# Inside the group or between two groups: where a small product, its decays and the sample fetches are placed in a hybrid recurrent step

## The chip, the cores and the metric

The kernel runs on one core of one Trainium2 chip. The metric is the device time of one execution in microseconds. Three runs of the kernel before gave 994.37, 994.74 and 998.79 us, median 994.74 us. A further execution was profiled, and every row of the trace comes from that one; its own time and its span are in the table below. One core has five engines with queues of their own: TensorE (PE, with its weight loads as PEld), VectorE (DVE), ScalarE (ACT), GpSimd (POOL) and SyncE (SP), which here only issues DMAs.

## The reference, cut to what matters

One step of a decoder trunk of two layers, for 256 prompt tokens and 8 sample sequences of 8 tokens, in float32:

```python
# layer 0
proj = einsum('btd,de->bte', rmsnorm(x), w_in)       # 2048 -> qkv, b, a, z_a, q_b, k_b, v_b, lr_b, z_b
qkv  = silu(causal_conv4(qkv, conv_a))               # 3072 columns
beta = sigmoid(b_raw); g = -exp(a_log) * softplus(a_raw + dt_bias)
o_a, S_a = gated_delta_rule(q_a, k_a, v_a, g, beta, S_a)          # 8 heads, chunked
gk   = log_sigmoid(einsum('btr,rk->btk', lr_b, w_lr) + b_lr) / 16
o_b, S_b = gla(q_b, k_b, v_b, gk, S_b)                            # 4 heads, chunked
x   += einsum('bte,ed->btd', concat(norm(o_a)*silu(z_a), norm(o_b)*silu(z_b)), w_out)
# layer 1
x   += RG-LRU(conv4(w_x rmsnorm(x))) * silu(w_g rmsnorm(x)) @ w_out
return rmsnorm(x), all new states (delta, gla, lru, conv) of prompt and samples
```

Three parts of this matter here. The narrow columns of `w_in`, 16 of `lr_b` and 8 each of `b_raw` and `a_raw`, make a product 32 columns wide, the small group. From it come the gates `g` and `beta` of the delta rule and, over `w_lr`, the decays `gk` of the gated linear attention (GLA). And every sample sequence has a state of its own (8 sequences x 8 heads of 128x128 for delta, x 4 heads of 128x256 for GLA), which is read, updated with the sample's keys and values, and written back.

## The kernel before, in words

**The dense products.** All 320 tokens (256 prompt, 64 sample) lie as columns, features on the 128 partitions. The wide weights are cut into groups of 512 output columns; a group has 8 weight loads of 512 KB (`wst`, three buffers) and four accumulators `acc` in PSUM of 128x320. Each weight tile is split into a rounded part `wh` (L239, ScalarE) and a rest `wl` (L240, VectorE), each input into `xh` and `xl`, and multiplied in three matmuls: xh with wh, xh with wl, xl with wh (L264). There are 5760 such matmuls; where the text says "a product" or counts products, it means one of them. When a group's accumulator is complete, its `evac` reads it out: for the groups of the convolution VectorE multiplies by the row scale `rb` into `slab` (L354, L355, `evac_padded`), and four taps make `yc` (L463). `rb` is 1/rms of each token; it comes from a chain over all of `x` (`start_work`, `row_rstd`, with L342 and L346), and some of the constants for it and for later come in `tables` (`pa`, `pc`, `dta`, `pb`, over SP's queue).

**What sets the order.** `run_group` walks the products; between them it calls `slot`, which lets one step of each work queue go on: `hi`, `lo` and `tails` hold generators, and a generator's `wait("name")` lets as many slots pass as the table `WAITS` says. The order of the instructions of each engine follows from where the generators' steps fall between the products, and from priorities that a scheduler uses on top. SP's DMAs are tied to the last product before them by `behind`.

**The border of groups 2 and 3.** (Groups counted from 1.) After the second group the program lets `hi` run until the row scale is in use ("start" done), then calls `small_group()`: 16 float32 matmuls of 32 columns into `smacc` (L490, 32 records in the trace), and on VectorE `sm` (L492, and a copy L494). The pool `start_p` is closed, and `lo` receives `small_work()` and behind it `gla_decays()`. `small_work` transposes `sm` (`smt`, L503), makes the gates, sums them up over the tokens with six short matmuls (`cum`, L533 to L538) and takes exponentials. `gla_decays` makes `gk`: `sml` (L1188), `lrp`, exponentials, a scan. Being behind `small_work` in the same queue, it starts when that has ended.

**The samples.** `sample_states` runs over the heads. `fetch` (L996) loads the rows for the update from scratch in DRAM into a tile of 96 partitions, three copies of the same 32 rows, by one DMA with a source of [0, 3], [4w, 32], [1, n*w]: `uk` and `uv` (192 KB) for delta, `uvk` (288 KB) for GLA. VectorE casts them (L1003), GpSimd takes the rests (L1007) and spreads them over four sequences (`uvm`, L1012), TensorE multiplies (`sn` L1112 for delta, `gsn` L1126 for GLA) and VectorE adds to the state (`ust` L1116, `ugt` L1130).

**GLA's output** goes through `gla_out`: squares on ScalarE (L1164), a power on GpSimd (`gso`), `gon` on VectorE (L1169), two transposes `got` on TensorE (L1173).

The functions and the calls:

Of the kernel before, what the change touches and what calls it, by code (L numbers as in the profile page):

```python
# [65 lines left out]
def wait(name):  # L66
    for _ in range(WAITS[name]):
        yield
# [3 lines left out]
def hybrid_step(ctx, tc, x_cols, w_dense, w_small, w_lr, w_gate, par_a, par_b, par_c, gains, head_rows,  # L72
# [3 lines left out]
    pe, act, dve, pool, sp = nc.tensor, nc.scalar, nc.vector, nc.gpsimd, nc.sync  # L76
# [36 lines left out]
    hi, lo, tails = [], [], []  # L113

    def advance(queue):
        while queue:
            try:
                next(queue[0])
                return True
            except StopIteration:  # L120
                queue.pop(0)
        return False
# [3 lines left out]
    def behind(i):  # L126
        tc.add_manual_dep(i.ins, marks[-1].name, mybir.DependencyInfo(
            mybir.DependencyClass.NoSync, mybir.DependencyReason.DATA), reason="issue_after")
# [12 lines left out]
    def slot0(n_lo=1):  # L141
        advance(hi)
        for _ in range(n_lo):
            advance(lo)
        advance(tails)

    def drain(queue):
        while advance(queue):
            pass
# [267 lines left out]
    def until(flag):  # L417
        while flag not in env["done"]:
            assert advance(lo) or advance(hi) or flag in env["done"], flag
# [76 lines left out]
    def small_work():  # L496

        yield from wait("small_work.4")
        ws = env["ws"]
# [487 lines left out]
    def sample_states(first, last):  # L987
# [5 lines left out]
        def fetch(name, src, off, n, w, bufs):  # L993

            t = ws.tile([R, n, w], F32, name=name, tag=name, bufs=bufs)
            behind(sp.dma_start(t.rearrange("p q w -> p (q w)"), bass.AP(  # L996
                tensor=src.tensor, offset=src.offset + off, ap=[[0, 3], [4 * w, 32], [1, n * w]])))
            return t
# [180 lines left out]
    def gla_decays():  # L1179

        gk = env["gk"] = env["lay0b"].tile([P, 4, NT], F32, name="gk")
# [625 lines left out]
    def shut(*pools):  # L1807
        for p_ in pools:
            p_.__exit__(None, None, None)
# [23 lines left out]
    small_group()  # L1833
    shut(start_p)
    lo.extend([small_work(), gla_decays()])
# [29 lines left out]
    drain(tails)  # L1865
    drain(lo)
# [52 lines left out]
    for m, f, n in ((0, 0, 1), (0, 1, 1), (0, 2, 2), (1, 0, 2), (1, 2, 2), (2, 0, 2), (2, 2, 2), (3, 2, 2)):  # L1919
        t = ob[m][:, f:f + n]  # L1920
# [64 lines left out]
```

## Time and profile before

| | before |
|---|---|
| runs | 994.37, 994.74, 998.79 us; median 994.74 |
| profiled execution | 994.33 us, span 992.6 us, mean granted clock 0.995 |
| TensorE busy | 969.5 us (98%) |
| VectorE, ScalarE, GpSimd busy | 707.5 (71%), 532.9 (54%), 220.2 us (22%) |
| longest groups | L264 with xh,wh 601.2, with xl,wh 595.1, with xh,wl 594.5 us (1920 matmuls each; the records overlap) |
| L240 `wl` on VectorE | 479, 726 ns each, 332.3 us |
| L239 `wh` on ScalarE | 479, 623 ns each, 278.7 us |
| DMA | 171.62 MB, mean 173 GB/s |

How to read it: busy times of matmuls are modelled and overlap, so that what TensorE really costs is read from start to start, and its idle time from the list of waits. A row of a timeline gives the start, the duration, engine, line, operation, the tile that is written and those that are read, shapes, the count, and in brackets the idle time before it with what ended that. A row of the chain of waits gives start, duration and what the end of the run was waiting for at that point.

### The profile page before, as it was taken

What the parts mean: (1) busy time and instruction counts of PE and PEld (TensorE: products, weight loads), DVE (VectorE), ACT (ScalarE), POOL (GpSimd) and SP (SyncE); (2) the same over time, 40 slices, a digit from 0 to 9 for tenths busy, and PEclk for the clock granted to TensorE, in tenths of its full rate; (3) what the DMA queues carried; (4) which work ended last, traced back from release to release, by engine and by line L of the source; (5) the groups of instructions that cost most, each with busy time, mean ns of one, the idle gap of its engine ahead of it and who ended that gap; (6) DMA issues with size and microseconds to landing.
All of it is one profiled execution on the core that took longest, in us unless ns stands there. A gap on an engine that the chain in (4) does not pass through costs nothing.

```text
span 992.6 us, 18768 instructions
## 1 busy us (share of the span) xinstructions
PE 969.5 (98%) x6917; PEld 950.5 (96%) x6917; DVE 707.5 (71%) x1485; ACT 532.9 (54%) x1083; POOL 220.2 (22%) x365
## 2 busy tenths in 40 slices
PE   9999999999999999999998999999999999999995
PEld 9989999999999999999978999999999999999995
DVE  7898887666545556779667789877969668766753
ACT  8556874457333444776423345447685885333441
POOL 4520018503282111120104234200010000052200
PEclk9999999999999999999999999999999999999998
DMA  8544444534455366445486877654545445568742
GB/s 297 178 134 135 133 130 157 143 131 135 127 157 163 93 218 228 133 111 151 157 258 204 241 258 229 228 165 146 158 124 189 130 127 169 165 216 276 258 155 106
DMA packets 64792, 171.62 MB, mean 173 GB/s; under 512 B 16345, under 2 KB 21997, under 8 KB 64189
## 3 DMA queue, kind: packets, MB, share of 16 engines
q1 hardware_dynamic: 59716, 160.35, 51.8%
q0 software_dynamic: 2720, 8.66, 2.3%
q10 hardware_dynamic: 2264, 1.42, 0.5%
q8 instruction: 54, 0.88, 0.4%
q14 instruction: 38, 0.30, 0.1%
HBM read 155.73 MB, written 14.68 MB: 172 GB/s over the span
## 4 chain that ended last, share of the span: by engine, by line
PE 44%; DVE 2%; DMA 2%; POOL 1%; issue 1%; SPq 0%; DVEq 0%; ACT 0%; POOLq 0%
PE acc L264 42%; DMA uv<-wv_scratch 1%; DMA ugt<-in_state_gla_dram 1%; POOL uvkh L1007 1%; DVE wl L240 1%; DVE ob L1921 0%; PE lg L1549 0%; PE lg L1550 0%; PE lg L1548 0%; PE gsn L1126 0%; PE sn L1112 0%; DVE xh L1410 0%; PE fsp L1670 0%; POOL gso L1166 0%; SPq L996 0%
## 5 line engine op out<-in xcount | busy, mean ns | idle before, releaser
L264 PE MATMUL acc<-xh,wh 128*128 128x320 f32 x1920 | 601.2, 313 | 2.7 <-DVE slab L355 1.2
L264 PE MATMUL acc<-xl,wh 128*128 128x320 f32 x1920 | 595.1, 310 | 1.3 <-DVE xl L1411 1.3
L264 PE MATMUL acc<-xh,wl 128*128 128x320 f32 x1920 | 594.5, 310 | 1.7 <-DVE wl L240 1.5
L239 ACT ACTIVATE wh<-wst 128x512 fp32r<-128x512 f32 x479 | 278.7, 623 | 312.5 <-PE acc L264 252.0
L240 DVE TENSOR_TENSOR wl<-wst,wh 128x512 fp32r<-128x512 f32 x479 | 332.3, 726 | 146.2 <-ACT wh L239 143.8
L264 PEld LDWEIGHTS acc<-xh,wh 128*128 128x128 f32 x1920 | 361.6, 188 | 6.0 <-issue 1.9
L264 PEld LDWEIGHTS acc<-xl,wh 128*128 128x128 f32 x1920 | 361.6, 188 | 3.4 <-DVE xl L1411 1.8
L264 PEld LDWEIGHTS acc<-xh,wl 128*128 128x128 f32 x1920 | 360.8, 188 | 3.5 <-DVE wl L240 2.8
L463 DVE SCALAR_TENSOR_TENSOR yc<-slab,pa,yc 128x344 f32<-128x344 f32 x72 | 42.6, 606 | 1.5 <-ACT yc L101 1.1
L698 POOL TENSOR_TENSOR xi<-xi,tmp 128x60 f32<-128x60 f32 (+24 forms) x62 | 26.2, 423 | 4.8
L1577 POOL MEMSET aa<- 128x32 f32 x4 | 0.7, 164 | 117.7 <-ACT rr L1564 66.7
L696 POOL TENSOR_TENSOR tmp<-ab,xi 128x60 f32<-128x60 f32 (+24 forms) x62 | 24.6, 398 | 4.9
L1007 POOL TENSOR_TENSOR uvkh<-uvk,uvkh 32x256 fp32r<-32x256 f32 (+1 forms) x8 | 12.2, 1526 | 58.3 <-DMA ugt<-in_state_gla_dram 51.0
L1012 POOL TENSOR_TENSOR uvm<-uvh,rm 96x512 fp32r<-96x512 f32 x16 | 20.9, 1327 | 1.6 <-PE sn L1112 1.3
L753 POOL TENSOR_TENSOR so<-so,mhalf 128x4 f32<-128x4 f32 x4 | 4.5, 1121 | 71.9 <-DVE so L752 71.9
L467 ACT ACTIVATE qkv<-yc 128x256 f32<-128x256 f32 x24 | 10.0, 416 | 18.7 <-DVE yc L463 18.6
L1116 DVE SCALAR_TENSOR_TENSOR ust<-ust,es,sn 128x128 f32<-128x128 f32 x64 | 17.7, 338 | 2.9 <-PE sn L1112 1.8
L101 ACT ACTIVATE yc<-slab,pa 128x344 f32<-128x344 f32 x24 | 13.3, 576 | 10.9 <-DVE slab L355 10.7
L1508 DVE SCALAR_TENSOR_TENSOR yc<-slab,pb,yc 128x344 f32<-128x344 f32 x32 | 17.5, 572 | 0.7 <-ACT yc L1506 0.6
L1119 POOL DMA_DIRECT2D out_s_delta_dram<-ust x8 | 6.0, 751 | 53.9 <-DVE ust L1116 53.9
L1130 DVE SCALAR_TENSOR_TENSOR ugt<-ugt,ebs,gsn 128x256 f32<-128x256 f32 x32 | 14.1, 472 | 4.3 <-PE gsn L1126 4.3
L354 DVE TENSOR_TENSOR slab<-acc,rb 128x256 f32<-128x256 f32 x36 | 14.9, 415 | 2.8 <-PE acc L264 2.6
(463 smaller groups left out, 1006.8 us busy)
## 6 DMA issues: line engine op xcount, KB each, us to landing
wst<-in_w_dense_dram SPq DMA_DIRECT2D x237, 512.0 KB
st<-in_state_delta_dram SPq DMA_DIRECT2D x8, 512.0 KB
st<-in_state_gla_dram SPq DMA_DIRECT2D x4, 1024.0 KB
ust<-in_state_delta_dram SPq DMA_DIRECT2D x8, 512.0 KB
out_s_delta_dram<-ust POOLq DMA_DIRECT2D x8, 512.0 KB, 5.1
ugt<-in_state_gla_dram SPq DMA_DIRECT2D x8, 512.0 KB
out_s_gla_dram<-ugt POOLq DMA_DIRECT2D x8, 512.0 KB, 5.0
x0r<-in_x_cols_dram SPq DMA_DIRECT2D x8, 320.0 KB
```

Source lines behind the costliest of these rows:

```text
L239: act.activation(h, wst[i][:, a, :], AF.Copy)
L240: env["last_split"] = dve.tensor_sub(l, wst[i][:, a, :], h.bitcast(F32))
L264: mm = pe.matmul(o, (h, h, l)[j][:, fs], (xh, xl, xh)[j][k], start=(k == 0 and j == 0), stop=(k == KT - 1 and j == 2))
L354: dve.tensor_mul(xp[:, 3:259], xp[:, 3:259] if acc is None else acc[:, :256], rb[:, :256])
L463: dve.scalar_tensor_tensor(y[:, :n], xp[:, j:j + n], pa[:, ft, j:j + 1], y[:, :n], op0=OP.mult, op1=OP.add)
L696: behind(pool.tensor_mul(tv, ab[:, j, j + 1:, None].to_broadcast([P, m, w]), xi[:, j:j + 1, :w].to_broadcast([P, m, w])))
L698: behind(pool.tensor_add(xi[:, j + 1:, :w], xi[:, j + 1:, :w], tv))
L1007: pool.tensor_sub(o, t[rows, :, cols], o.bitcast(F32))
L1012: pool.tensor_mul(m, src.bitcast(F32)[:, None, :].to_broadcast([R, 4, P]), rm4[:R, :, None].to_broadcast([R, 4, P]))
L1116: dve.scalar_tensor_tensor(s_, s_, es[:, col:col + 1], ps[:, b, :], op0=OP.mult, op1=OP.add)
L1130: dve.scalar_tensor_tensor(s_, s_, ebs[:, h, 4 * hb + b + i:4 * hb + b + i + 1], ps[:, i * 256:(i + 1) * 256], op0=OP.mult, op1=OP.add)
L1508: dve.scalar_tensor_tensor(y[:, :n], xp[:, j:j + n], pb[:, ft, 2 + j:3 + j], y[:, :n], op0=OP.mult, op1=OP.add)
```

## The change

Four things change together.

1. `small_group()` and the closing of `start_p` move out of the gap between the second and third group into `small_work()`, which begins with a new wait of 10 slots. So the 16 matmuls stand inside the third group.
2. `gla_decays()` gets a queue of its own, `lo2`, which `slot` advances once per slot beside the others. `small_work` puts it there before the first `smt`, and it begins with a new wait of 14 slots.
3. `fetch` issues three DMAs of 32 rows in place of one of 96. SP issues 36 of them where it issued 12.
4. Numbers in `WAITS`: the two new names, and other values for `small_work`, `gla_decays`, `masks`, `tables`, `sample_states`, `delta_sample`, `gla`, `quad_out`, `evac_res_sumsq`, `fill` and `resid`.

```diff
 WAITS = {
-    "small_work.1": 0, "small_work.2": 1, "small_work.3": 6,
+    "small_work.1": 0, "small_work.2": 2, "small_work.3": 10,
+    "small_work.1": 0, "small_work.2": 2, "small_work.3": 10,
-    "quad_out.1": 7, "delta_sample.7": 10, "delta_sample.5": 8,
+    "quad_out.1": 10, "delta_sample.7": 4, "delta_sample.5": 4,
-    "gla_decays.1": 16, "gla_decays.2": 8, "gla_decays.4": 10, "gla_decays.6": 0, "gla.3": 2, "gla.4": 20,
+    "gla_decays.1": 12, "gla_decays.2": 7, "gla_decays.4": 1,  "gla_decays.6": 3, "gla.3": 3, "gla.4": 16,
-    "evac_res_sumsq.1": 4, "fill.2": 14, "resid.1": 15, "sample_states.1": 9, "sample_states.14": 7,
+    "evac_res_sumsq.1": 0, "fill.2": 11, "resid.1": 7,  "sample_states.1": 8, "sample_states.14": 10,
-    "tables.1": 10, "masks.1": 5, "masks.3": 2,
+    "tables.1": 14, "masks.1": 1, "masks.3": 0, "small_work.5": 10, "gla_decays.8": 14,
...
-    hi, lo, tails = [], [], []
+    hi, lo, lo2, tails = [], [], [], []
...
         for _ in range(n_lo):
             advance(lo)
+        advance(lo2)
         advance(tails)
...
     def small_work():
 
+        yield from wait("small_work.5")
+        small_group()
+        shut(start_p)
         yield from wait("small_work.4")
+        lo2.append(gla_decays())
         ws = env["ws"]
         ps = bank("smt")
...
             t = ws.tile([R, n, w], F32, name=name, tag=name, bufs=bufs)
-            behind(sp.dma_start(t.rearrange("p q w -> p (q w)"), bass.AP(
-                tensor=src.tensor, offset=src.offset + off, ap=[[0, 3], [4 * w, 32], [1, n * w]])))
+            rows = bass.AP(tensor=src.tensor, offset=src.offset + off, ap=[[4 * w, 32], [1, n * w]])
+            for c in range(3):
+                behind(sp.dma_start(t[32 * c:32 * c + 32].rearrange("p q w -> p (q w)"), rows))
             return t
...
     def gla_decays():
 
+        yield from wait("gla_decays.8")
         gk = env["gk"] = env["lay0b"].tile([P, 4, NT], F32, name="gk")
...
     while "start" not in env["done"]:
         advance(hi)
-    small_group()
-    shut(start_p)
-    lo.extend([small_work(), gla_decays()])
+    lo.append(small_work())
```

The new lines shift the numbers: L264 is L265 in the changed kernel, L490 is L491, L996 is L1003.

What moves on the engines. First TensorE around the border of the second and third group; `xh_104` begins a group's inputs. Before:

```order
L264 MATMUL acc<-xl_135,wh 128x320
L264 MATMUL acc<-xh_119,wl 128x320
L490 MATMUL smacc<-ob_136,smw 32x320 x4
L490 MATMUL smacc<-ob_137,smw 32x320 x4
L490 MATMUL smacc<-ob_138,smw 32x320 x4
L490 MATMUL smacc<-ob_139,smw 32x320 x4
L264 MATMUL acc<-xh_104,wh 128x320
...
L264 MATMUL acc<-xh_104,wl 128x320
L503 MATMUL smt<-quart,sm 128x32 x2
L264 MATMUL acc<-xh_105,wh 128x320
```

In the change, in the third group:

```order
L265 MATMUL acc<-xl_122,wh 128x320
L265 MATMUL acc<-xh_106,wl 128x320
L491 MATMUL smacc<-ob_136,smw 32x320 x4
L491 MATMUL smacc<-ob_137,smw 32x320 x4
L491 MATMUL smacc<-ob_138,smw 32x320 x4
L491 MATMUL smacc<-ob_139,smw 32x320 x4
L265 MATMUL acc<-xh_107,wh 128x320
...
L265 MATMUL acc<-xh_107,wl 128x320
L508 MATMUL smt<-quart,sm 128x32 x3
L265 MATMUL acc<-xh_106,wh 128x320
```

The small product stood ahead of the third group's first product and now stands behind 33 of its products; nine more follow up to `smt`, where there were fifteen.

Second, VectorE from the reciprocal of the row scale (`rb_84` is rb) to the two splits around the six taps. Before:

```order
L342 RECIPROCAL rb_84<-rb_84 128x320
L240 TENSOR_TENSOR wl<-wst,wh 128x512 x3
L354 TENSOR_TENSOR slab<-slab,rb_84 128x256
L355 TENSOR_TENSOR slab<-slab,rb_84 128x8x8
L354 TENSOR_TENSOR slab<-slab,rb_84 128x256
L355 TENSOR_TENSOR slab<-slab,rb_84 128x8x8
L240 TENSOR_TENSOR wl<-wst,wh 128x512
L463 SCALAR_TENSOR_TENSOR yc<-slab,pa,yc 128x344 x6
L240 TENSOR_TENSOR wl<-wst,wh 128x512
```

In the change:

```order
L343 RECIPROCAL rb_84<-rb_84 128x320
L241 TENSOR_TENSOR wl<-wst,wh 128x512 x2
L355 TENSOR_TENSOR slab<-slab,rb_84 128x256
L356 TENSOR_TENSOR slab<-slab,rb_84 128x8x8
L355 TENSOR_TENSOR slab<-slab,rb_84 128x256
L356 TENSOR_TENSOR slab<-slab,rb_84 128x8x8
L355 TENSOR_TENSOR slab<-slab,rb_84 128x256
L241 TENSOR_TENSOR wl<-wst,wh 128x512
L464 SCALAR_TENSOR_TENSOR yc<-slab,pa,yc 128x344 x6
L241 TENSOR_TENSOR wl<-wst,wh 128x512
```

Of the splits, two instead of three stand between the reciprocal and the first slab that needs rb.

Third, SP's queue where it loads the tables; `pb` feeds `nclam`, which stands on VectorE ahead of the reciprocal. Before:

```order
L209 DMA wst<-in_w_dense_dram 128x1024
L1761 DMA pa<-in_par_a_dram 128x672
L209 DMA wst<-in_w_dense_dram 128x1024 x2
L1761 DMA pc<-in_par_c_dram 128x7
L1761 DMA dta<-in_head_rows_dram 128x16
L209 DMA wst<-in_w_dense_dram 128x1024 x2
L1761 DMA pb<-in_par_b_dram 128x688
L209 DMA wst<-in_w_dense_dram 128x1024
L1783 DMA xt_scratch<-same 128x4x128
```

In the change:

```order
L210 DMA wst<-in_w_dense_dram 128x1024
L1768 DMA pa<-in_par_a_dram 128x672
L1790 DMA xt_scratch<-same 128x4x128
L210 DMA wst<-in_w_dense_dram 128x1024 x2
L1768 DMA pc<-in_par_c_dram 128x7
L1768 DMA dta<-in_head_rows_dram 128x16
L210 DMA wst<-in_w_dense_dram 128x1024
L1768 DMA pb<-in_par_b_dram 128x688
```

`pb` comes one weight load earlier, and the scratch write of 256 KB, which came two places behind `pb`, now comes ahead of it.

More of the change, by code (lines that the diff above doesn't have):

```diff
@@ L418, in until @@
         while flag not in env["done"]:
-            assert advance(lo) or advance(hi) or flag in env["done"], flag
+            assert advance(lo) or advance(lo2) or advance(hi) or flag in env["done"], flag
     def evac_conv_a(slot_name, half, part):
@@ L1865, in hybrid_step @@
     drain(tails)
+    drain(lo2)
     drain(lo)
```

24 rows, old and new, of the table WAITS are left out of this document.

## The prediction

> **What bounds the kernel now.** I read the page's first part, then the groups of TensorE's waits, then the stretches around the longest waits, and last the chain that ended last. The page says which engine counts:
>
> ```profile
> PE 969.5 (98%) x6917; PEld 950.5 (96%) x6917; DVE 707.5 (71%) x1485; ACT 532.9 (54%) x1083; POOL 220.2 (22%) x365
> ```
>
> TensorE is busy for 98% of the 992.6 us span. The number of its instructions is the same in both kernels, so only its waits, its clock and the two ends can change. The chain gives the price of one product when nothing disturbs it, 4.41 / 30 = 0.147 us:
>
> ```profile
> 534.88 4.41 PE acc L264 x30
> ```
>
> The waits of TensorE (total us, times, longest) are the list of what can be won:
>
> ```profile
> PE got L1173 <- DVE gon L1169: 2.3, 4, 0.7
> PE acc L264 <- DVE wl L240: 1.5, 2, 0.7
> PE gsn L1126 <- POOL uvm L1012: 1.3, 1, 1.3
> PE acc L264 <- DVE xl L1411: 1.3, 2, 0.8
> PE acc L264 <- DVE slab L355: 1.2, 1, 1.2
> PE acc L264 <- DVE xh L1410: 1.1, 2, 0.8
> PE smt L503 <- DVE sm L492: 0.9, 1, 0.9
> PE cum L533 <- DVE gt L526: 0.7, 1, 0.7
> PE acc L264 <- DVE ob L1453: 0.2, 1, 0.2
> ```
>
> These add up to 10.5 us, about 1% of the run. The changed lines touch four places: the border of groups 2 and 3 (slab 1.2, smt 0.9, cum 0.7, one of the two wl waits), the first fetch of sample operands (xl, xh), the later fetches (gsn, the other wl) and, through renumbered slots, the tail of the gated linear attention (got). The clock is the fifth. In the stretches the columns are busy us of PE, PEld, DVE, ACT and POOL, then the granted clock, the DMA share and GB/s:
>
> ```profile
> 60.00:80.00 20.00, 17.73 (x136) 15.62 (x135) 18.19 (x47) 14.96 (x33) 2.90 (x6) 1.00 0.51 152
> 80.00:100.00 20.00, 19.31 (x121) 18.49 (x120) 17.16 (x51) 11.43 (x23) 0.74 (x2) 0.91 0.38 117
> ```
>
> **Part 1: the small product inside the group.** TensorE before, at the border, and VectorE, which feeds it:
>
> ```profile
> 65.06 2.36 PE L490 MATMUL smacc<-ob,smw 128*32 128x320 f32 x32
> 68.63 0.38 PE L264 MATMUL acc<-xh,wh 128*128 128x320 f32 x1 [1.21 <-DVE slab L355]
> 71.99 0.63 PE L503 MATMUL smt<-quart,sm 128*128 128x32 f32 x4 [0.93 <-DVE sm L492]
> ```
> ```profile
> 39.84 0.18 DVE L1781 TENSOR_SCALAR nclam<-pb 128x16 f32<-128x16 f32 x1 [2.34 <-DMA pb<-in_par_b_dram]
> 55.80 0.42 DVE L354 TENSOR_TENSOR slab<-slab,rb 128x256 f32<-128x256 f32 x1 [1.32 <-POOL rb L346]
> 56.74 0.69 DVE L240 TENSOR_TENSOR wl<-wst,wh 128x512 fp32r<-128x512 f32 x1
> 57.35 3.01 DVE L463 SCALAR_TENSOR_TENSOR yc<-slab,pa,yc 128x344 f32<-128x344 f32 x6
> 60.27 0.69 DVE L240 TENSOR_TENSOR wl<-wst,wh 128x512 fp32r<-128x512 f32 x1
> 67.93 0.42 DVE L354 TENSOR_TENSOR slab<-acc,rb 128x256 f32<-128x256 f32 x1
> ```
>
> The 2.36 us of small matmuls stay, 33 products later, so they cost the same. What goes is their cover: they ran while VectorE caught up with the slab that must leave PSUM before group 3 may start. The wait was 1.21 us behind that cover; without it, and with VectorE as late as now, it would be 3.6 us. How late VectorE is hangs on when the row scale rb is there (55.80). In the new order one split (L240) fewer stands ahead of that point, and that split, which TensorE needs 42 products ahead of the border (65.06 - 42 x 0.147 = 58.9), stands behind six yc. From the rb point it takes two slab pairs 0.94, half a pair 0.34, a split 0.60, the six yc 2.92 and itself 0.60: 5.4 us. If rb comes d earlier, it ends at 61.2 - d. Then follow, up to the freed bank, about 7.1 us of the same kinds (five splits 3.0, six yc 3.0, two and a quarter slab pairs 1.1): 68.3 - d.
>
> The loads of the tables move one weight load up in SP's queue, so the 2.34 us wait for pb shrinks, and the chain behind it to rb moves with it. That bounds d: 0 to 2.3. With d = 2.3 TensorE stalls nothing at the split and 1.0 at the border, together 1.0; with d = 0 it is 2.3 + 0.9 = 3.2. Then sm: in the new order ten yc (5.0), four splits (2.4), three slab pairs (1.4) stand between the first bank and sm (0.5), 9.3 us; TensorE does 42 products and the 2.36 us in that time, 8.5 us, so it waits 0.8, and up to 1.5 if the third smt waits for the copy behind sm. Against 1.21 + 0.93 = 2.1 before, the place gives -0.2 (d = 2.3, sum 1.9) to +2.4 (d = 0, smt 1.3, sum 4.5). The cum wait (0.69, one of the rows above) now has a longer lead: 0 to -0.7. The early wl wait (0.7) sits where masks and splits swap: 0 to -0.7. I take +1.1 for the place (d = 1.2) and -0.35 for each of the other two: **+0.4 us**, between -1.6 and +2.4. Outside both ends: pb might land later, since a scratch write of 256 KB also moves up; that is the rival D.
>
> **Part 2: the lane of its own for the decays.** No instruction is added on TensorE. The sml, lrp and cum matmuls keep their lengths; they only shift by tens of products, in a stretch where VectorE is at 17.16 of 20. Their work is needed only when the attention starts, many groups later, and ScalarE's one additional activation-table load has the idle 46% of that engine to lie in. Cost 0; without that cover (a waiting lrp ahead of the products on TensorE's queue) 0.7 each, the cum row's size. The stretch also holds the clock loss:
>
> ```profile
> 89.31 0.40 PE L533 MATMUL cum<-gt,umask 128*128 128x16 f32 x2 [0.69 <-DVE gt L526]
> 91.94 0.46 PE L264 MATMUL acc<-xh,wl 128*128 128x320 f32 x1
> 92.20 0.47 PE L264 MATMUL acc<-xh,wh 128*128 128x320 f32 x1
> 95.38 0.31 PE L264 MATMUL acc<-xh,wh 128*128 128x320 f32 x1
> 95.53 0.31 PE L264 MATMUL acc<-xl,wh 128*128 128x320 f32 x1
> ```
>
> Products start 0.26 us apart at 91.94 and 0.15 apart at 95.38. Over these 3.4 us some 13 products cost 0.12 each too much, 1.5 us. It follows the short cum and sml matmuls with their wait. They stay together, so I count 0, between -1.5 (gone) and +1.5 (a second such stretch). [...]
>
> **Part 3: the fetch by 32 rows.** Twelve loads become 36. The chain that ended last and VectorE's waits show what the old ones do:
>
> ```profile
> 510.55 0.80 SPq L996
> 511.39 11.29 DMA uv<-wv_scratch
> ```
> ```profile
> 522.77 0.42 DVE L1003 CAST uvh<-uv 96x512 fp32r<-96x512 f32 x1 [1.84 <-DMA uv<-wv_scratch]
> 523.11 0.32 DVE L1410 CAST xh<-ob 128x320 fp32r<-128x320 f32 x1
> 524.35 1.39 DVE L1410 CAST xh<-ob 128x320 fp32r<-128x320 f32 x1
> 871.37 0.56 DVE L1003 CAST uvkh<-uvk 96x768 fp32r<-96x768 f32 x1 [4.80 <-DMA uvk<-vk_scratch]
> ```
> ```profile
> 862.39 0.72 SPq L996 DMA_DIRECT2D uvk<-vk_scratch  x1
> L739 SPq DMA_DIRECT2D XT<-xd_scratch x16: 303/430/504, 192.0 to 309.1; - x16
> xd_scratch<-xt POOLq DMA_DIRECT2D x8, 32.0 KB, 3.3
> out_s_delta_dram<-ust POOLq DMA_DIRECT2D x8, 512.0 KB, 5.1
> ```
>
> 192 KB take 11.3 us, and 288 KB 9.0 us (862.39 to 871.37), while 512 KB elsewhere take 5.1. No 96-row load is near the others, so the shape is slow, not the size. A piece of 64 or 96 KB lies between the rows of 32 KB (3.3) and 512 KB (5.1): I take 3.5, with 5.1 as the slow end. Three issues at 0.43 each (L739) put the last piece 0.9 after the first: landing 4.4 us after the first issue, 6.0 at the slow end, instead of 9 to 11.3. SP pays 3 x 0.43 - 0.72 = 0.6 us more per fetch, 7 us in twelve places; SP mostly waits for buffers there, so 0, and 0.6 each where a weight load behind them is late. [...]
>
> At 523 to 531: uv lands near 517 instead of 522.7, VectorE's block of 1.84 us goes, and the four waits of xl and xh (2.4) with the ob wait after them shrink. They don't all go: the second xh took 1.39 instead of 0.32 while GpSimd worked beside it, and that work now comes earlier but still beside the splits. From -2.6 to 0; I take **-1.8**, since the blocked 1.84 us is the first cause in the order of time. At 879:
>
> ```profile
> 872.15 5.96 POOL L1007 TENSOR_TENSOR uvkh<-uvk,uvkh 32x256 fp32r<-32x256 f32 x2 [51.02 <-DMA ugt<-in_state_gla_dram]
> 878.18 2.35 POOL L1012 TENSOR_TENSOR uvm<-uvkh,rm 96x512 fp32r<-96x512 f32 x2
> 879.27 0.50 PE gsn L1126 x2
> ```
>
> The cast comes at 867 instead of 871.4, GpSimd's chain ends 4.6 us earlier, and gsn also stands nine products (1.3 us) later. The 1.3 us wait goes with slack: **-1.3** (0 if GpSimd really waits for ugt, which the row names; its operands are uvk alone, so I hold that for the latest semaphore). The second wl wait (0.7) lies beside the last uk and uv fetches: **-0.4**, 0 to -0.7.
>
> **Part 4: the other slots.** The four got waits come from a chain over ScalarE, GpSimd and VectorE; got and what it waits for both move by about ten products. 0 to -0.6, or +0.3 if one lands closer: **-0.2**. The tail after 970 us is not moved.
>
> **Sum.** +0.4 - 1.8 - 1.3 - 0.4 - 0.2 = -3.3 us, made against the profiled execution, 994.33 us with a span of 992.6: 991.0. The median of the runs is 0.4 above that execution; I leave 991.0.
>
> **Rivals.**
> A, the forecast: 990 to 993.5.
> B, everything moves the right way: the start ends at its good end (-1.6), all four fetch waits go (2.6 + 1.3 + 0.7 = -4.6), got -0.6, and no sparse stretch trips the clock (-1.5). -8.3, 986.0; with one or two of these missing 987 to 989. For it: each has a row that names its cause. Against it: waits on a full VectorE tend to reappear next door.
> C, the new fetches land no earlier, or GpSimd's pace and not the landing sets the waits: +0.4 - 0.2, and 0.4 saved by the later gsn: 994. For it: GpSimd's 5.96 us pair at 872; against it: 1.84 and 4.80 us of VectorE waiting for exactly these loads.
> D, slower: the row scale comes late. With VectorE at 18.19 of 20 us every us by which rb falls behind 55.80 is a us of idle TensorE, at the split and then at the border without its old cover. The cause would be pb or a weight load queued behind the 256 KB scratch write. At d = -3 the start costs +5.4 - 0.7, the fetches bring -2.5: 996.5. It eats the gains of 3.7 from d = -2 on (4.4 - 0.7), and with fetches at -2.5 the kernel would be measurably slower from d of about -6.
>
> **How the numbers follow.** About 0.5%, 5 us, is what a measurement can tell from no change: below 989.8 or above 999.7. A 0.46 (a fifth of it below 989.8), B 0.27, C 0.13, D 0.14 (0.06 of all above 999.7). Faster 0.36, same 0.58, slower 0.06. The likeliest time is 991.0. The range from 986.5 to 995.5 leaves out the best end of B and the bad half of D; A's own is 990 to 993.5.
>
> **What would show it.** Right: the gsn wait and VectorE's waits for uv and uvk are gone from their lists; the xl and xh waits are under 1 us; one new wl wait before 60 us, and 0.5 to 1.5 us at the border of group 3. Wrong: uv still lands 8 us or more after its first issue (C); rb's slab later than 55.8 us (D); granted clock 1.00 from 80 to 100 (towards B), or another stretch of 0.26 us spacing (towards D).

## The result, and the profile after

| | before | after |
|---|---|---|
| median of the runs, us | 994.56 (993.98 to 998.79, 6 runs) | 988.31 (987.04 to 989.39, 6 runs) |
| ratio, 95% interval | 1 | 0.9929 (0.9911 to 0.9947) |
| profiled execution, us | 994.33 | 988.05 |
| its span, us | 992.6 | 985.9 |

The changed kernel is faster by 6.3 us, 0.6%. The predicted 991.0 us was 2.7 us too high; the range held the time. TensorE's waits after the change (total us, times, longest; three more, at the two ends of the run, are left out, as they are in the prediction's list: they are nearly the same in both kernels):

```profile
PE acc L265 <- DVE wl L241: 3.2, 2, 2.0
PE got L1179 <- DVE gon L1175: 1.2, 2, 0.6
PE cum L538 <- DVE gt L531: 0.6, 1, 0.6
PE nbt L669 <- ACT dtm L633: 0.4, 1, 0.4
PE y L943 <- DMA XT<-xt_scratch: 0.2, 1, 0.2
```

The waits for xl, xh, ob, slab, sm and for GpSimd's uvm are gone, two of four got waits too. New are a longer wl wait and two small ones. To see where the time went, the 5760 matmuls of line L264 (L265) can be counted through in both traces: all are there, and from number 140 on in the same order (before that, 15 places hold another of the three kinds). The start times of a few of them, and below them how much each stretch got shorter or longer against before:

```
matmul no.          1500    2816    2900    3400    3600    5100    5200    5759
before, starts    268.57  517.20  533.46  609.43  641.54  875.56  892.57  977.77
after, starts     270.36  517.35  529.91  605.64  636.72  870.75  886.12  971.14

stretch          to 1500 to 2816 to 2900 to 3400 to 3600 to 5100 to 5200 to 5759
after              +1.8    -1.6    -3.7    -0.2    -1.0     0.0    -1.6    -0.2
e1 fetch only      -1.9    -0.2    -3.5     0.0    +0.2     0.0    -1.6    -0.2
e2 old fetch       +1.1    -2.0    -1.4    -0.2    -1.0     0.0    -0.3     0.0
e3 old start       -0.6    -0.7    -3.7    -0.2    -1.1     0.0    -1.6    -0.2
e6 inside, no lane +10.6   -0.3    -3.7    -0.2    -1.1     0.0    -1.6    -0.2
e7 lane only       -0.8    -2.1    -3.7    -0.2    -1.1     0.0    -1.6    -0.2
e9 inside, lane    +2.5    -2.0    -3.7    -0.2    -1.1     0.0    -1.6    -0.2
```

The first column is the start with the border of groups 2 and 3 and the delta work up to 270 us, the second the attention's tail, the third the first fetch of sample operands, the fifth the later delta fetches, the seventh the GLA fetches. The rows e1 to e9 are the experiments below. The start lost 1.8 us; every other stretch gained or stayed. Each row is one profiled execution, and the first column also differs between executions of the same code: e2 and e6 have a wait of 1.7 and 1.3 us for the first weights near 8 us, while after, with the code of e2 at that place, has none.

Two places of the trace after carry that. The start, TensorE and VectorE:

```profile
60.78 0.42 PE L265 MATMUL acc<-xh,wl 128*128 128x320 f32 x1 [2.03 <-DVE wl L241]
```
```profile
38.29 0.85 DVE L1788 TENSOR_SCALAR nclam<-pb 128x16 f32<-128x16 f32 x1
49.13 2.14 DVE L343 RECIPROCAL rb<-rb 128x320 f32<-128x320 f32 x1
55.23 0.42 DVE L355 TENSOR_TENSOR slab<-slab,rb 128x256 f32<-128x256 f32 x1 [2.29 <-POOL rb L347]
57.11 3.01 DVE L464 SCALAR_TENSOR_TENSOR yc<-slab,pa,yc 128x344 f32<-128x344 f32 x6
60.04 0.69 DVE L241 TENSOR_TENSOR wl<-wst,wh 128x512 fp32r<-128x512 f32 x1
```

pb is there 1.5 us earlier (nclam at 38.29 instead of 39.84), but rb only 0.6 us (55.23 instead of 55.80). The split behind the six yc ends at 60.7, and TensorE has waited 2.0 us for it. The granted clock in five stretches of 3.41 us around this wait and around the cum matmuls (columns as in the prediction; the clock is the third number from the end):

```profile
58.44:61.85 3.41, 1.38 (x10) 1.11 (x9) 3.41 (x10) 2.73 (x7) 0.00 (x0) 1.00 0.03 10
61.85:65.26 3.41, 3.41 (x15) 3.41 (x14) 3.41 (x8) 2.75 (x8) 0.00 (x0) 0.50 0.73 199
65.26:68.67 3.41, 3.41 (x25) 3.41 (x24) 3.41 (x9) 2.22 (x6) 2.48 (x4) 1.00 0.56 167
92.57:95.98 3.41, 2.82 (x20) 2.09 (x19) 2.80 (x11) 2.18 (x3) 0.00 (x0) 1.00 0.62 166
95.98:99.39 3.41, 3.41 (x15) 3.41 (x15) 2.84 (x6) 0.63 (x1) 0.00 (x0) 0.50 0.05 4
```

In the first stretch TensorE works 1.38 of 3.41 us; in the next it has exactly half its clock, and does 15 matmuls instead of 25. The same happens behind the cum matmuls. Before there was one such stretch, now there are two. At 0.12 us for each of 13 matmuls, as read from the rows of before, one costs 1.5 to 1.6 us (an estimate), which is most of the start's +1.8.

### The profile page after: what moved, and what is told of

It reads as the page before. It is cut to its first block, busy times and chain, and to the rows that moved or that the text cites. A ratio compares the mean times of both kernels' runs of the same rounds, so it can differ in the third digit from the quotient of the medians.

```text
span 985.9 us, 18789 instructions
## 1 busy us (share of the span) xinstructions
PE 968.4 (98%) x6917; PEld 951.9 (97%) x6917; DVE 708.9 (72%) x1485; ACT 534.7 (54%) x1084; POOL 216.6 (22%) x365
## 4 chain that ended last, share of the span: by engine, by line
PE 86%; DVE 4%; ACT 3%; issue 3%; DMA 2%; POOL 1%; SPq 0%; DVEq 0%; ACTq 0%; POOLq 0%
PE acc L265 75%; DVE wl L241 1%; ACT wh L240 1%; DMA wst<-in_w_dense_dram 1%; DMA XT<-xt_scratch 1%; DVE ob L1927 0%; POOL xsums L1782 0%; PE gpo L1368 0%; PE lg L1556 0%; PE lg L1557 0%; PE lg L1555 0%; DVE yc L464 0%; PE gsn L1132 0%; PE po L844 0%; PE sn L1118 0%
## 5 line engine op out<-in xcount | busy, mean ns | idle before, releaser
L265 PE MATMUL acc<-xh,wh 128*128 128x320 f32 x1920 | 602.0, 314 | 0.2 <-ACT wh L231 0.2
L265 PE MATMUL acc<-xh,wl 128*128 128x320 f32 x1920 | 595.2, 311 | 3.2 <-DVE wl L241 3.2
L265 PE MATMUL acc<-xl,wh 128*128 128x320 f32 x1920 | 596.3, 311 | 0.0
L265 PEld LDWEIGHTS acc<-xh,wl 128*128 128x128 f32 x1920 | 361.7, 189 | 4.2 <-DVE wl L241 3.7
L265 PEld LDWEIGHTS acc<-xh,wh 128*128 128x128 f32 x1920 | 362.1, 189 | 2.8 <-issue 1.3
L265 PEld LDWEIGHTS acc<-xl,wh 128*128 128x128 f32 x1920 | 362.5, 189 | 1.4
L1013 POOL TENSOR_TENSOR uvkh<-uvk,uvkh 32x256 fp32r<-32x256 f32 (+1 forms) x8 | 8.4, 1049 | 57.2 <-DMA uvk<-vk_scratch 48.1
```

Source lines behind the costliest of these rows:

```text
L265: mm = pe.matmul(o, (h, h, l)[j][:, fs], (xh, xl, xh)[j][k], start=(k == 0 and j == 0), stop=(k == KT - 1 and j == 2))
```

## The experiments

Medians and ratios are against runs of the kernel before on the same chip. The experiments ran on three chips and at different times; the median of before was 994.86 us beside e1 to e4, 994.15 beside e5 to e8, 995.43 beside e9 and e10, and 994.78 beside e11. Between these groups a difference of medians can therefore be off by about 1 us, and the ratios are the better comparison; their intervals reach 0.0014 to 0.0021 (1.4 to 2.1 us) to either side.

### e1: the fetch alone

```diff
--- before
-            behind(sp.dma_start(t..., ap=[[0, 3], [4 * w, 32], [1, n * w]])))
+            for c in range(3):
+                behind(sp.dma_start(t[32 * c:32 * c + 32]..., ap=[[4 * w, 32], [1, n * w]]))
```

> The kernel before with the fetch by 32 rows alone; every slot, the small group and the decays stay. Theory F (the 96-row form of the load is slow, and that alone caused the waits at 523 and 879): uv lands within 5 us of its first issue, VectorE's waits for uv and uvk go, the time falls by about 6 us, to 987.5 to 990. Theory O (the new slots put the casts behind the input splits and gsn nine products later, and that is the gain): at most 2 us of gain, 992.5 or more, and waits remain at 523.

Measured: 988.4 us against 994.86, ratio 0.9931 (0.9917 to 0.9946). One edit of the four gives as much as all of them. VectorE waits neither for uv nor for uvk any more; at matmuls 2816 to 2900 3.5 us are gained, at 5100 to 5200 1.6 us. TensorE's longest waits in this kernel are those of the unchanged parts:

```profile
PE got L1174 <- DVE gon L1170: 2.3, 4, 0.7
PE acc L264 <- DVE wl L240: 1.5, 2, 0.8
PE acc L264 <- DVE slab L355: 1.2, 1, 1.2
```

The wl wait near 622 us stays (0.8): it was not the fetch's. And the start is 1.9 us shorter here than before, though its code is the same. The trace says why: the half-clock stretch behind cum did not come in this execution (clock 1.00 from 80 to 100 us). That is 1.5 to 1.6 of the 1.9 us. So as much of the 6.5 us between the two medians may be that; the fetch itself is 3.5 + 1.6 = 5.1 us by the stretches.

### e2: the change with the old fetch

```diff
--- after
-            for c in range(3):
-                behind(sp.dma_start(t[32 * c:32 * c + 32]..., ap=[[4 * w, 32], [1, n * w]]))
+            behind(sp.dma_start(t..., ap=[[0, 3], [4 * w, 32], [1, n * w]])))
```

> The changed kernel with the old fetch of one 96-row DMA; slots, small group and decays as changed. Theory F: uv and uvk land 9 to 11 us after issue again, the waits come back near 523, 627 and 879, and the time is 993.5 to 996, no better than before since the start lost about 1.3 us. Theory O: 988.5 to 991, with the casts waiting but TensorE not.

Measured: 990.69 us, ratio 0.9964 (0.9949 to 0.9978). Neither theory has all of it: the time lies where theory O puts it, 4 us better than before, but TensorE waits again, which only theory F says, and less than F says. VectorE waits for the loads again:

```profile
DVE uvkh L1008 <- DMA uvk<-vk_scratch: 3.3, 1, 3.3
DVE uvh L1008 <- DMA uv<-wv_scratch: 2.3, 1, 2.3
DVE ukh L1008 <- DMA uk<-kt_scratch: 0.9, 1, 0.9
```

TensorE's part in that is 1.5 us for xl and 1.1 for ob at 886 us. By the stretches the slots alone gain 1.4 us at the first fetch (alone the fetch gains 3.5, together 3.7), 1.0 at 600 to 640 us (the fetch alone none), 2.0 in the attention's tail (the fetch alone none), and 0.3 at 879. So the two edits overlap at the first fetch and at the GLA fetches: each removes some of the same waits. That is why the parts, 6.5 and 4.2, don't add up to the whole, 6.3.

### e3: the change with the old start

```diff
--- after
-        yield from wait("small_work.5")
-        small_group()
-        shut(start_p)
         yield from wait("small_work.4")
-        lo2.append(gla_decays())
...
-        yield from wait("gla_decays.8")
...
-    lo.append(small_work())
+    small_group()
+    shut(start_p)
+    lo.extend([small_work(), gla_decays()])
```

with the old numbers of small_work, gla_decays, masks and tables.

> The changed kernel with the start put back: the small group between groups 2 and 3, the decays behind small_work in the same queue, and the old numbers of small_work, gla_decays, masks and tables. Fetch and all other slots as changed. Theory S (the start of the change costs 1.3 us net: a 2.0 us wait for a weight split behind the six taps and a second half-clock stretch of 1.5 us outweigh the border's waits): 986.5 to 987.5, one half-clock stretch and the border's two waits back. Rival (the moved small group pays, and what looked lost is given back later): 989 or more.

Measured: 985.6 us (four runs, 984.61 to 987.1), ratio 0.9907 (0.9890 to 0.9925), 2.7 us better than the whole change by the medians and 2.2 by the ratios, whose intervals overlap, and a little better than theory S said. The border's two waits are back (1.2 and 0.9), the 2.0 us wait is gone, and there is one half-clock stretch, at 91 us (clock 0.91 from 80 to 100 us).

### e4: one DMA of 96 rows with an outer count of 96

```diff
--- after
-            rows = bass.AP(..., ap=[[4 * w, 32], [1, n * w]])
-            for c in range(3):
-                behind(sp.dma_start(t[32 * c:32 * c + 32]..., rows))
+            behind(sp.dma_start(t..., bass.AP(..., ap=[[w, 96], [1, n * w]])))
```

> The changed kernel with one DMA of 96 distinct rows per fetch, whose source counts 96 in its outer dimension instead of 3 by 32 (the rows overlap in the scratch, so the sample updates compute with other operands; sizes and instructions are the same). Theory F1 (what is slow is the outer count of 3 on the source side, not one load of 96 rows or its 192 KB): uv lands within 5 us, time within 1 us of the changed kernel, 987.5 to 989. Rival F2 (a single DMA of that size is slow, three in parallel are not): uv lands 8 us or later and the time is 993 or more.

Measured: 987.13 us, ratio 0.9922 (0.9906 to 0.9939). VectorE has no wait for a fetch, and the three fetch stretches gain 3.6, 1.1 and 1.6 us, the same as with three DMAs. The load, from its trace, where one of the four has a landing time:

```profile
uvk<-vk_scratch SPq DMA_DIRECT2D x4, 288.0 KB, 6.2
```

6.2 us from issue to landing for one load of 288 KB, where the form of 3 by 32 rows took 9.0 us before, from its issue to the cast that uses it. So neither the size nor the number of rows nor the number of DMAs made it slow; the source's outer dimension of 3 did. That the same 32 rows are read three times is not it either, since the three DMAs of e1 read them as often. The traces' records of single packets show what differs between the old form and the split one: the 96 packets of 3 KB of one uvk fetch run 2.5 to 2.8 at a time over 5.0 to 6.0 us in before, and 6.4 to 10.9 at a time over 1.8 to 3.8 us in after. Why an outer count of 3 keeps so few of them under way, no run shows. The two additional issues per fetch cost nothing that can be seen (e4 0.9922, after 0.9929). The load landed at 6.2 us; the expectation said 5 for uv, whose landing is not in the trace, so that its number was probably too low.

### e5, e6, e7: the three parts of the start, each alone on e3

```diff
--- e3
-    "masks.1": 5, "masks.3": 2, "tables.1": 10,
+    "masks.1": 1, "masks.3": 0, "tables.1": 14,                          # e5
...
+        yield from wait("small_work.5"); small_group(); shut(start_p)      # e6, in small_work
-    small_group(); shut(start_p)                                           # e6, between the groups
...
+        lo2.append(gla_decays())                                           # e7, in small_work
-    lo.extend([small_work(), gla_decays()])
+    lo.append(small_work())                                                # e7
```

> The kernel of e3_old_start (985.6 us) plus only the changed numbers of masks and tables (masks.1 5 to 1, masks.3 2 to 0, tables.1 10 to 14). Theory S1 (the start's loss comes from these numbers: they let the row scale's chain start earlier in VectorE's queue than its data come, so a weight split that TensorE needs lands behind the six taps): the wait of about 2 us before 62 us comes back with its half-clock stretch, 987.5 to 989. Rival S2 (the loss comes from the small group inside the group): no such wait, 985 to 986.3.

> The kernel of e3_old_start plus only the small group inside the third group (with the new small_work numbers); decays stay behind small_work. Theory S1: no 2 us wait before 62 us; the border's wait of 1.2 us stays or grows to 2.5 as its cover shrinks, the smt wait goes: 985 to 986.5. Rival S2: 987.5 or more.

> The kernel of e3_old_start plus only the lane of its own for the decays with their new numbers. Both theories: no change on TensorE's waits of more than 0.5 us, 985 to 986.3. A gain of more than 1 us would say that the decays had held up the attention's start; a loss of more than 1 us that they collide with VectorE's work before 120 us.

Measured: e5 986.42 us, ratio 0.9920 (0.9900 to 0.9941); e6 996.01 us, 1.0006 (0.9991 to 1.0020); e7 984.42 us, 0.9897 (0.9878 to 0.9916).

e5 has the wait as theory S1 says, and the half-clock stretch behind it:

```profile
PE acc L265 <- DVE wl L241: 3.3, 2, 2.2
60.00:80.00 20.00, 19.03 (x136) 17.48 (x137) 19.83 (x52) 15.29 (x36) 3.98 (x8) 0.91 0.49 146
```

But the loss is 0.8 us by the medians (1.3 by the ratios) and not 2 to 3, since TensorE, which is now late at the border, finds the bank free there, and the border's two waits (1.2 and 0.9) are gone. The loss moved more than it grew. So S1 names where the long wait comes from, but not where all of the 2.7 us went.

e6 fits neither theory: it loses 10 us against e3, far more than the whole start of the change. Its profile is 11.2 us later than that of e3 at matmul 1500. The border is a small part of it: one wait of 2.3 us in place of 1.2 and 0.9. The rest comes later and in pieces: two more half-clock stretches (behind the border, clock 0.91 from 60 to 80 us, and at 219 us; the mean granted clock of the execution is 0.991, that of e3 0.995; 3.1 us at the price above), 1.8 us before a small matmul of the delta rule at 218 us, whose cause the trace does not name, four waits of 0.3 to 0.4, the 1.3 us for the first weights, and waits for slab, the longest of them this:

```profile
203.68 0.38 PE L265 MATMUL acc<-xh,wh 128*128 128x320 f32 x1 [1.89 <-DVE slab L356]
202.97 0.42 DVE L355 TENSOR_TENSOR slab<-acc,rb 128x256 f32<-128x256 f32 x1 [3.67 <-POOL slab L383]
200.19 0.20 POOL L702 TENSOR_TENSOR xi<-xi,tmp 128x8 f32<-128x8 f32 x1
202.65 0.29 POOL L383 COPY slab<-pa 128x96 f32<-128x96 f32 x1
```

GpSimd copies the margins into the slab of the next group (L383), and these stand in its queue behind a chain of triangular inverses of the delta rule (xi and the operations around it). These belong to work that stands in the queue `lo` behind small_work and the decays. With the small product inside the group all of that comes later, and GpSimd passes the lateness on to a dense group, here 1.9 us. That the other pieces behind the border come from the same lateness is likely, since of them e9 below has only one wait of 0.4, but the trace of e6 does not show it for each. The scan of the decays shows the shift: 109.3 to 119.2 us in e3, 123.6 to 129.0 in e6.

e7 lies 0.6 us below its expectation: the lane alone gains 1.2 us against e3 by the medians and 1.0 by the ratios, and the intervals overlap, so that this gain is not shown. In its trace the two waits that e3 had between 270 and 320 us (0.5 each) are not there. But e5, with the decays behind small_work as in e3, has only 0.15 us of them, so they can't be put down to the decays' place.

### e8: the cum matmuls one slot apart

```diff
--- e3
-    "small_work.3": 6,
+    "small_work.3": 40,
...
-        pe.matmul(ps[:, 0:16], umask, gt[:, 0:16], start=True, stop=True)
-        pe.matmul(ps[:, 16:20], u8mask, gt[:, 16:20], start=True, stop=True)
+        behind(pe.matmul(ps[:, 0:16], umask, gt[:, 0:16], start=True, stop=True))
+        yield
+        behind(pe.matmul(ps[:, 16:20], u8mask, gt[:, 16:20], start=True, stop=True))
+        yield
...
```

> The kernel of e3_old_start with the six short cum matmuls one slot apart, three products between two of them, and 34 slots later, so that their gates are there. Theory H (the half-clock stretch at 91 us comes from a window that these short matmuls and their 0.7 us wait leave too empty): no half-clock stretch between 80 and 110 us, the cum wait gone, 984 to 985.2. Rival (a stretch falls there whatever the work is): the granted clock of that stretch still shows 0.91, and the time stays at 985.6 within 0.5.

Measured: 994.97 us, ratio 1.0002 (0.9989 to 1.0016), 9.4 us worse than e3 by the medians, which neither theory says. Between 80 and 100 us it does what H says, clock 1.00 and TensorE busy throughout. The loss is at 174 us, with the mechanism of e6:

```profile
173.75 0.60 PE L265 MATMUL acc<-xh,wh 128*128 128x320 f32 x1 [6.32 <-DVE slab L356]
173.05 0.42 DVE L355 TENSOR_TENSOR slab<-acc,rb 128x256 f32<-128x256 f32 x1 [8.14 <-POOL slab L383]
170.41 2.33 POOL L697 TENSOR_TENSOR ab<-ab,bn 128x1024 f32<-128x1024 f32 x1 [16.92 <-DMA ab<-bd_scratch]
172.75 0.27 POOL L383 COPY slab<-pa 128x96 f32<-128x96 f32 x1
160.00:180.00 20.00, 13.68 (x76) 13.45 (x75) 9.46 (x21) 6.94 (x15) 8.49 (x18) 0.83 0.47 103
```

34 slots more in small_work, and GpSimd waits 16.9 us for a load of the late delta work with the margin copies behind it. Here this is nearly the whole loss: the wait of 6.3 us and a half-clock stretch of 6.8 us that it ends in (about 3 us, at twice the price of one) make 9.3.

### e9 and e10: the same two with the lane

```diff
--- after, for e9
-    "tables.1": 14, "masks.1": 1, "masks.3": 0,
+    "tables.1": 10, "masks.1": 5, "masks.3": 2,
--- e7, for e10
+    the spread cum matmuls of e8, "small_work.3": 44
```

> The changed kernel with the old numbers of masks and tables: small group inside, lane for the decays, fetch by 32 rows, all other new slots. With e6 (inside without lane, 996.0 us) and e7 (lane without inside, 984.4 us) it completes the square. Theory L (inside the group the small product delays small_work; without the lane the decays and with them all later work in that queue come late, and GpSimd's in-order queue passes that on to the dense groups; the lane takes this away): no waits for slab at 170 to 205 us, the border's wait about 2.3 us with a half-clock stretch behind it, 985 to 987.5. Rival (the inside place itself costs the 10 us): 992 or more.

> The kernel of e7_decay_lane (984.4 us) with the six cum matmuls spread as in e8, three products apart, and late enough that their gates are there. Theory L: the 6.3 us wait for slab at 174 us of e8 does not come back, since the decays no longer stand behind small_work: 983 to 985. Theory H: no half-clock stretch between 85 and 110 us and no cum wait. Rival (the late gates themselves hold up the quads, lane or not): 988 or more with a slab wait between 160 and 210 us.

Measured: e9 988.07 us, ratio 0.9924 (0.9910 to 0.9939), a little above its expectation; e10 984.92 us, 0.9893 (0.9876 to 0.9909). No wait for slab between 160 and 210 us in either. The square of medians in us, with the ratios (three chips):

| | decays behind small_work | decays in a lane |
|---|---|---|
| small product at the border | 985.6, 0.9907 (e3) | 984.4, 0.9897 (e7) |
| small product inside the group | 996.0, 1.0006 (e6) | 988.1, 0.9924 (e9) |

So theory L holds in its mechanism: by the ratios the lane is worth 8 us once the small product is inside, and alone 1 us, within the noise. The place inside still costs 2.7 us by the ratios with the lane, and 3.4 by the spans of the two profiles. In the profile of e9 are two half-clock stretches (none in e7, clock 1.00 from 60 to 100 us): one behind cum and one behind the border, where TensorE now waits 2.3 us in one piece:

```profile
60.00:80.00 20.00, 17.63 (x120) 15.04 (x120) 17.82 (x47) 11.83 (x31) 2.89 (x6) 0.91 0.48 139
80.00:100.00 20.00, 19.38 (x122) 18.56 (x121) 16.01 (x50) 13.26 (x22) 0.34 (x2) 0.91 0.37 116
PE acc L265 <- DVE slab L356: 2.3, 1, 2.3
```

What the changed kernel loses against e3 needs no more than the small product's place: e9 has the old numbers of masks and tables and the same time as the change, 988.1 and 988.3. The numbers by themselves make a wait of the same length at another place (e5); both together do not make two. e10 has no half-clock stretch (clock 1.00 from 60 to 120 us) and no cum wait, as H says, but its time is the same as that of e7 within the noise, which had no such stretch in its profile either.

### e11: the border filled

```diff
--- e9
+    fill = bank("fill")
+    for _ in range(8):
+        behind(pe.matmul(fill[:, :P], ones, ones, start=True, stop=True))
     lo.append(small_work())
```

> The kernel of e9_inside_with_lane (988.1 us, a wait of 2.3 us at the border and a half-clock stretch right behind it) with eight float32 matmuls of ones by ones into a spare bank at the border, which nobody reads; they add work and no result. Theory H2 (the half-clock stretch comes from what TensorE does not do in the 3.4 us before it): the idle time at the border falls below 1 us, the granted clock of 60 to 80 us is 1.00, and the time falls by about 1.5 us, to 986 to 987, though work was added. Rival (the stretch follows from something else at that place, such as the narrow matmuls): clock 0.91 there still, time 988 or more.

Measured: 986.48 us, ratio 0.9914 (0.9900 to 0.9928), faster than e9 with work added, by 1.6 us of the medians and 1.0 of the ratios (overlapping intervals, another chip):

```profile
64.94 1.95 PE L1842 MATMUL fill<-ones 128*128 128x128 f32 x16
68.61 0.38 PE L265 MATMUL acc<-xh,wh 128*128 128x320 f32 x1 [1.72 <-DVE slab L356]
60.00:80.00 20.00, 18.28 (x142) 16.01 (x140) 19.53 (x50) 12.99 (x33) 2.88 (x6) 1.00 0.45 143
```

The first product of group 3 starts at the same time (68.61, in e9 68.37), the idle time before it fell only from 2.3 to 1.7 us, not below 1 as expected, but the half-clock stretch is gone from this place. The one behind cum is missing in this profile too (clock 1.00 from 80 to 100 us, in e9 0.91), so the stretch to matmul 1500 shrank by 1.9 us, a little more than one of them. So H2 is right about the clock, though its own condition was not met. It is not one execution alone: the mean granted clock of the six runs of e11 is 0.996 or 0.997, that of e9 0.993 to 0.995. Why the stretch behind cum went as well, with nothing changed there, is open. With no stretch at half clock e11 is still 1.4 us later at matmul 1500 than e7 (269.15 and 267.75), so that part of the price of the place inside is not the clock.

In the profile after, the stretches last 3.41 us and the two start 34.1 us apart. In the 3.41 us before the first of them TensorE was busy for 1.38 us.

## Why the prediction was right or wrong

**What bounds the kernel, right.** What was won and lost lies in TensorE's waits and its clock: between the two ends of the run its idle time fell from 11.1 us in 17 waits to 5.7 us in 8, and one more stretch at half clock was added.

**The price of a wait, mis-sized.** This failed most. The prediction took the idle time of a wait's row as its price: 2.6 us for the five at 523 to 531, and a gain of 1.8, since it held that some would stay. The stretch gained 3.7. Of the 1.9 that are missing, 0.8 is the waits that were to stay and went, and 1.1 is the price. The rows of before show it:

```profile
523.00 0.31 PE L264 MATMUL acc<-xh,wl 128*128 128x320 f32 x1
523.57 0.38 PE L264 MATMUL acc<-xh,wh 128*128 128x320 f32 x1 [0.26 <-DVE xh L1410]
```

From start to start it is 0.57 us, 0.42 more than the undisturbed 0.147, while the row says 0.26 idle. Idle time counts from the modelled end of the matmul before (0.31 after its start), and an undisturbed successor would have started 0.16 earlier. So this wait costs its idle time and 0.16 us; the other four cost 0.16 to 0.24 more. From start to start the five make 3.6 us for 2.6 idle, and the products right behind three of them start another 0.1 late each: 3.9 in all. At 879 it is 1.3 idle and 1.5 from start to start, and the stretch gained 1.6.

**Part 3, the fetch.** That the form of the load and not its size makes it slow was right (e1, e4), rival C wrong. The term at 879 held: -1.3 said, -1.6 measured. The landing was too optimistic: 4.4 us after the first issue was said, and a single piece of 64 KB took about 6 where the trace of the changed kernel has a landing:

```profile
uk<-kt_scratch SPq DMA_DIRECT2D x12, 64.0 KB, 6.1
uv<-wv_scratch SPq DMA_DIRECT2D x12, 64.0 KB, 5.8
```

It did not matter, as the casts come later. The wl wait near 627 us went as said (-0.4 said, -1.0 measured), but for another reason: the slots and not the fetch remove it (e1 +0.2, e2 -1.0).

**Part 4, the other slots, mis-sized.** -0.2 said, -1.6 measured in the attention's tail. Got and the work before it were seen to move by the same ten products, and the prediction concluded that the waits stay. Two of the four went, and with them a wait of 0.4 for y (L830) that the prediction's list leaves out; another of 0.2 for y came. It also took the new slots around the first fetch for neutral, while alone they gain 1.4 us there.

**Part 1, the border: mechanism right, outcome by another path.** The split behind six yc was said to end at 61.2 - d; with d = 0.6 it ended at 60.7, and the wait of 2.0 us lies between the two that were worked out. The forecast for the border itself (0.9 to 1.0, then 0.8 to 1.5 at smt) was wrong: both waits are 0. At the border that is because TensorE came 1.5 us later by the half clock; the bank was free at about 67.7, where the prediction's sum has it for d = 0.6. At smt it is not the clock, since e11 at full clock has no wait there either: VectorE has sm ready at 77.4, just when TensorE comes. The step that failed is the second stretch of half clock, which was counted at 0 with +1.5 as its bound; it came. The early wl wait was said to shrink from 0.7 and grew to 1.1.

**Part 2, the lane, wrong.** Costed at nothing, "their work is needed only when the attention starts". That is about right for the lane alone (e7), but not beside the small product inside, where it is worth 8 us (e6, e9). What was overlooked is not who needs the decays but who stands behind them in the same queue: the delta rule's work, and behind that on GpSimd the margins of the next dense group. Parts 1 and 2 were priced one by one, and there the prediction had luck: the place inside alone would have cost 10 us and not 1.1, and the lane, priced at 0, took 8 of them back.

**The sum.** Said +0.4 - 1.8 - 1.3 - 0.4 - 0.2 = -3.3; measured by the stretches +1.8 - 3.7 - 1.6 - 1.0 - 1.6 and -0.4 in two others, -6.6 of span. The likeliest time's own range, 990 to 993.5, missed by 1.7 us; the wide range held, with some luck, since a start that was 1.4 us worse than said stands against gains that were 4 to 5 us better. Of the rivals D did not come (rb is earlier than 55.80), and B is nearest: all fetch waits went, but the start and the clock did not go its way. Of the signs that were named, those of the fetch came; the new wl wait came at 60.8 and not before 60, no wait is left at the border, and the second half-clock stretch, named as a sign towards D, came without D.

## What to carry to other kernels

Count a wait from start to start and not by its idle time: where matmuls overlap, each wait costs the overlap too, here 0.16 to 0.24 us for each of the five that were read. Look at the outer count of a DMA's source before its size: a repeated block of rows as the outer dimension made a load of 192 to 288 KB take 9 to 11 us from issue to use, and splitting it, or giving it an outer count of 96, was worth 5 us. When work is put into a queue of steps, ask what stands behind it there and in the queues of other engines (in e8 the margin copies stood behind a wait of 16.9 us in GpSimd's queue, and TensorE waited 6.3 us for the slab); the best versions measured here take the fetch, the lane and the other slots, and leave the small product at the border: e7 with 984.4 us, ratio 0.9897 (0.9878 to 0.9916) to before, and e10 with 0.9893. What the lane adds there is within the noise (e3, 0.9907).

## What the runs showed of the hardware

Between the first product and the last, the half-clock stretch lasted 3.41 us in before and both times in after, and 6.8 us in e8, behind a wait of 6.3 us. One of 3.41 us costs 1.5 to 1.6 us, by the estimate above. In after, e5, e6 and e9 one wait of 2.0 to 2.3 us in one piece at the start goes with a clock of 0.91 from 60 to 80 us; in before, e3, e7 and e10, with two waits of 1.2 and 0.9 us and products between them, that clock is 1.00. In e11, with a wait of 1.7 us and the added matmuls, it is 1.00 too. Behind the short cum matmuls the stretch came in five of nine profiles (before, after, e3, e6 and e9, clock 0.91 from 80 to 100 us; not in e1, e5, e7 and e11, 1.00) with code that is the same there or nearly so; what decides that, and whether a window left too empty is behind it, as theory H has it, no run shows. Whether it comes may explain a part of the spread, which is an inference. Of the 23 runs of before beside e5 to e8, which took 992.32 to 999.36 us, the five with a mean granted clock of 0.997 took 992.47 to 993.48, the four with 0.991 or 0.992 took 995.94 to 999.36. But in e1 and e5 the time of a run does not follow its clock (e1: 987.19 us at 0.995 and 988.66 at 0.997; e5: 985.61 at 0.994 and 987.54 at 0.997), so something else differs between executions too.
